# A hybrid decoder trunk: the first layer's splits cut into pieces, and both output projections moved from 256 to 512 columns a matmul

## The chip, the cores and the metric

The kernel runs on one core of a Trainium2 chip. The metric is the device time of one execution in microseconds (us). TensorE (PE in the profile) multiplies; its weight loads (PEld) are rows of their own and overlap the multiplications. VectorE is DVE, ScalarE is ACT, GpSimd is POOL, and SP issues most of the DMA transfers. Each engine works through its own instructions in order and waits on semaphores for the others.

## The reference, cut to what matters

The input is a sequence of 1024 rows of 1024 features in float32. Layer A is a gated DeltaNet, and layer B is a sliding-window attention whose keys and values come from the output of layer A. Both end in an output projection, `x + o @ w_out`, with `o` of 1024 x 2048 and `w_out` of 2048 x 1024. Layer A has 8 heads, and each is a recurrence over chunks of the sequence:

```python
def step(S, inp):
    qk_i, qd_i, kd_i, u_i, w_i, gl_i = inp
    v_new = u_i - jnp.einsum("bhck,bhkv->bhcv", w_i, S)
    o = jnp.einsum("bhck,bhkv->bhcv", qd_i, S) + jnp.einsum("bhcs,bhsv->bhcv", qk_i, v_new)
    S = S * gl_i[..., None, None] + jnp.einsum("bhck,bhcv->bhkv", kd_i, v_new)
    return S, o
```

`kd_i` are the keys times their decay to the chunk's end, and `qk_i` the products of queries and keys times their decay.

## The kernel before

**Split numbers.** A float32 product is made of three matmuls of a faster type (F32R): each operand is split into a rounded part `hi` and the rest `lo`, and hi*hi, hi*lo and lo*hi are added in one PSUM bank. The split of a large tile is one POOL instruction (hi) and one DVE instruction (lo = x - hi), in `split` (L645, L646).

**Layer A, head by head.** `head_delta` (front) writes the recurrence of head h, and the projections of the next head (`head_in`, lines L180, L182 and L184 in `gemm_ct`: 512 columns each) are woven into it as filler. The order of the PE is that of the code. The other engines' instructions are ordered when the program is built, by a scheduler that knows no measured time. A head takes some 104 us. Its parts, in order: the products of queries and keys (L666); an inversion on 64 x 64 blocks (L687, L694); `merge` (L756 to L767); and the scan over 8 chunks n = 0..7.

**The merge and the scan** are where the first half of the change lies. After the merge the decayed keys `kt` (multiplied by `kdec` on POOL in L681) are split into `kth` (tile `w0`) and `ktl` (buffer `lt`), and the products `dm` into `dmh` (tile `w1`) and `dml`. Every chunk then runs a chain over four engines: PE L802 -> ACT L804 (`vh`, buffer `Z`) -> DVE L805 (`vl`, buffer `lh`) -> PE L816 -> DVE L819 or L822 (state `S`) -> PE L793 -> DVE L795 -> PE L802 of the next chunk. L816 of chunk n reads `kth[:, n]`; L652 to L654 read `dmh` and `dml` of the chunk before. The load of the decays of a later head (`dm<-gd`, SP L603) waits for the last reader of the tile; POOL L608 and ACT L612 then work on what it brought.

**The queries** are split into `qh` and `ql` one head ahead, in the same way.

**The output projections** (`out_proj`, called once for each layer) go over 2 halves of the rows and 2 column blocks of 512. Four PSUM tiles, one for each 128 rows, are filled from 8 weight tiles of 512 KB. A weight tile holds 4 row blocks of 128 by 256 columns, and a matmul takes 256 columns:

```python
for kk in range(4):
    nc.tensor.matmul(po, oh[:, kk, ts], hi[:, kk, :], start=(k4 + kk + b == 0), stop=False)
    nc.tensor.matmul(po, oh[:, kk, ts], lo[:, kk, :], start=False, stop=False)
    nc.tensor.matmul(po, ol[:, kk, ts], hi[:, kk, :], start=False, stop=(k4 + kk + b == 7))
```

That is 2 x 2 x 8 x 4 x 4 x 3 = 1536 matmuls for a projection. `weight` loads a tile (SP L125) and splits it on POOL (L150) and DVE (L157), and `weights` names the tiles in order.

Of the kernel before, what the change touches and what calls it, by code (L numbers as in the profile page):

```python
# [7 lines left out]
F32 = mybir.dt.float32  # L8
# [5 lines left out]
ALU = mybir.AluOpType  # L14
# [4 lines left out]
P = 128  # L19
T = 1024  # L20
D = 1024
NB = T // P
# [42 lines left out]
class Kernel:  # L65
# [575 lines left out]
    def split(self, x, ph, hi, pl, lo):  # L641

        nc = self.nc
        hi, lo = (p.tile([P, NB, P], F32R, name=t, bufs=1) for p, t in ((ph, hi), (pl, lo)))
        nc.gpsimd.tensor_scalar(out=hi, in0=x, scalar1=1.0, scalar2=1.0, op0=ALU.mult, op1=ALU.mult)  # L645
        nc.vector.tensor_tensor(out=lo, in0=x, in1=self.f32(hi), op=ALU.subtract)  # L646
        return hi, lo

    def three(self, ps, wh, wl, mh, ml):

# [5 lines left out]
    def head_delta(self, h, H):  # L656
        nc, dl, sm, dps = self.nc, self.dl, self.sm, self.dps
        kq, kt, vt, dm = H.kq, H.kt, H.vt, H.dm
        sh = [P, NB, 64]

        lt = dl.tile([P, NB, P], F32, name="lt", bufs=1)
        for n2 in range(NB // 2):
            ps = dps.tile([P, 2, 2, P], F32, name="kqp")
            for c in range(2):
                n = n2 * 2 + c
                nc.tensor.matmul(ps[:, c, :, :], kq[:, n, 0, :], kq[:, n, :, :], start=True, stop=True)  # L666
            for c in range(2):
                n = n2 * 2 + c
# [7 lines left out]
        for r in (0, 64):  # L676
            nc.scalar.copy(out=lh[r:r + 64, :, :], in_=lt[r:r + 64, :, r:r + 64])
        nc.gpsimd.affine_select(out=lt, in_=lt, pattern=[[0, NB], [1, P]], compare_op=ALU.is_gt, fill=0.0, base=0,
                                channel_multiplier=-1)
        qh, ql = self.split(kq[:, :, 1, :], dl, "qh", dl, "ql")  # L680
        nc.gpsimd.tensor_tensor(out=kt, in0=kt, in1=self.kdec[:, :, h:h + 1].broadcast_to([P, NB, P]), op=ALU.mult)  # L681
        blocks = [(n, r) for n in range(NB) for r in (0, 64)]

        def prod(lhs, rhs):
# [81 lines left out]
            nc.tensor.matmul(ps[0:64, n, :], Zf[64:128, n, :], xt[64:128, n, 64:128], start=True, stop=True)  # L766
        nc.scalar.copy(out=xt[0:64, :, 64:128], in_=ps[0:64, :, :])  # L767
        yield WAIT["merge"]
        kth, ktl = self.split(kt, sm, "w0", dl, "lt")
        dmh, dml = self.split(dm, sm, "w1", dl, "dml")  # L770

        H.o = o = vt
        sso = sm.tile([P, NB], F32, name="sso")
# [15 lines left out]
        for n in range(NB):  # L789
            po[n % 2] = dps.tile([P, 2, 256], F32, name="kqp")  # L790
            if n:
                ps = dps.tile([P, 512], F32, name="sc")[:, 0:256]
                nc.tensor.matmul(ps, kq[:, n, 0, :], S, start=True, stop=True)  # L793
                r = sm.tile(wide, F32, name="r")
                nc.vector.scalar_tensor_tensor(out=r, in0=ps, scalar=self.neG[:, n, h:h + 1], in1=vt[:, n, :],  # L795
                                               op0=ALU.mult, op1=ALU.add)
                inside(n - 1)
                yield WAIT["row"]
            else:
                r = vt[:, n, :]  # L800
            ps = dps.tile([P, 512], F32, name="sc")[:, 0:256]
            nc.tensor.matmul(ps, xt[:, n, :], r, start=True, stop=True)  # L802
            beta = self.beta[:, n, h:h + 1]
            nc.scalar.activation(out=vh, in_=ps, func=AF.Copy, scale=beta)  # L804
            nc.vector.scalar_tensor_tensor(out=vl, in0=ps, scalar=beta, in1=self.f32(vh), op0=ALU.mult,  # L805
                                           op1=ALU.subtract)
            if n:
                self.three(po[n % 2][:, 0, :], qh[:, n, :], ql[:, n, :], Sh, Sl)
                nc.scalar.activation(out=o[:, n, :], in_=po[n % 2][:, 0, :], func=AF.Copy, scale=self.eG[:, n, h:h + 1])
            yield WAIT["new"]  # L810
            if n < NB - 1:
                ps = dps.tile([P, 512], F32, name="sc")[:, 0:256]
                nc.tensor.matmul(ps, kth[:, n, :], vh, start=True, stop=False)
                nc.tensor.matmul(ps, ktl[:, n, :], vh, start=False, stop=False)
                yield WAIT["low"]
                nc.tensor.matmul(ps, kth[:, n, :], vl, start=False, stop=True)  # L816
                S2 = sm.tile(wide, F32, name="S")
                if n:
                    nc.vector.scalar_tensor_tensor(out=S2, in0=S, scalar=self.egl[:, n, h:h + 1], in1=ps,  # L819
                                                   op0=ALU.mult, op1=ALU.add)  # L820
                else:
                    nc.vector.tensor_copy(S2, ps)  # L822
                S = S2
                nc.scalar.copy(out=Sh, in_=S)
                nc.vector.tensor_tensor(out=Sl, in0=S, in1=self.f32(Sh), op=ALU.subtract)
                yield WAIT["state"]
        inside(NB - 1)

# [68 lines left out]
    def out_proj(self, og, resid, cur, tiles, raws, px, acc, dst, finish):  # L897


        nc = self.nc  # L900
        for half in range(2):
            xs, nxt = [], []
            for cp in range(2):
                cs = slice(cp * 512, cp * 512 + 512)
                ps = [acc.tile([P, 2, 256], F32, name="acc") for _ in range(4)]
                for k4 in range(4):
                    oh, ol = cur[k4]
                    for b in range(2):
                        hi, lo = self.take()
                        if cp == 0 and (k4, b) == (2, 0):  # L910
                            self.flush()
                            for c in range(4):
                                xs.append(px.tile([P, D], F32, name="xo", bufs=4))
                                nc.sync.dma_start(xs[c], resid[half * 4 + c])
                        for c in range(4):
                            ts = slice(c * P, c * P + P)
                            po = ps[c][:, b, :]
                            for kk in range(4):
                                nc.tensor.matmul(po, oh[:, kk, ts], hi[:, kk, :], start=(k4 + kk + b == 0), stop=False)  # L919
                                nc.tensor.matmul(po, oh[:, kk, ts], lo[:, kk, :], start=False, stop=False)  # L920
                                nc.tensor.matmul(po, ol[:, kk, ts], hi[:, kk, :], start=False, stop=(k4 + kk + b == 7))  # L921
                                if kk % 2:
                                    self.tick()
                            if (k4, b) == (3, 1):
                                nc.vector.tensor_tensor(out=xs[c][:, cs], in0=ps[c].rearrange("p b c -> p (b c)"),
                                                        in1=xs[c][:, cs], op=ALU.add)
# [413 lines left out]
    def weights(self):  # L1340

        I = self.I
        rows = lambda name: I[name].rearrange("o (k p) c -> p (o k) c", p=P)
        bin_ = rows("b_w_in")
        col = lambda w, b, gain: (w[:, :, b * P:(b + 1) * P], [KT, P], gain)
        four = lambda w, k, c, gain: (w[:, 4 * k:4 * k + 4, c * 256:c * 256 + 256], [4, 256], gain)
        gain = lambda j: self.gcolb[:, 4 * j:4 * j + 4]
        for h in range(AH):
            for b in (8 + h, h, 16 + 2 * h, 17 + 2 * h):
                yield col(self.win, b, None)  # L1350
            if h == 0:
                yield col(self.win, 32, None)
            if h == 1:
                yield col(self.win, 33, None)
            for i in ([h - 1] if h > 1 and h - 1 not in self.late else []) + ([AH - 1, *self.late] if h == AH - 1 else []):
                for b in (32 + 2 * i, 33 + 2 * i):
                    yield col(self.win, b, None)
        for _ in range(2):
            for c in (0, 2):
                for k in range(4):  # L1360
                    for b in range(2):
                        yield four(rows("a_w_out"), k, c + b, None)
        wkv = I["w_kv"].rearrange("(k p) c -> p k c", p=P)
        for c in range(2):
            for k in range(2):
                yield four(wkv, k, c, gain(k))
        for kind, hg, j in self.b_order():
            if kind == "q":
                for k in range(2):
                    yield four(bin_, k, hg, gain(2 + k))  # L1370
            else:
                yield col(bin_, 16 + 2 * hg + j, self.gcolb[:, 8:16])
        for _ in range(2):
            for c in (0, 2):
                for k in range(4):
                    for b in range(2):
                        yield four(rows("b_w_out"), k, c + b, None)

    def dump(self, name, ap):
        self.nc.sync.dma_start(self.dbg[name], ap)  # L1380
# [21 lines left out]
```

## Time and profile before

| | |
|---|---|
| median of 3 runs | 1890.71 us (1887.74 to 1893.08) |
| the profiled execution: its time, its span in the trace | 1894.54 us, 1892.8 us |
| PE busy | 1829.7 us (97%) |
| PEld, DVE, ACT, POOL busy | 1567.2, 1239.6, 838.1, 512.6 us |
| TensorE clock granted, mean | 0.995 |
| projection of layer A | 899.5 to 1089.6 us of the span |
| projection of layer B | 1704.5 to 1888.8 us of the span |

Times inside the trace count from the span's start. A busy PE is not one at its peak: matmuls are pipelined and each shows a duration longer than its distance to the next, so cost is read from the starts of neighbouring rows.

### The profile page before, as it was taken

To read this page: it belongs to the slowest core of one execution; us is meant where nothing else is said; L and a number is where in the kernel's file an instruction comes from. 1 tells how busy PE (TensorE), PEld (TensorE's weight loads), DVE (VectorE), ACT (ScalarE), POOL (GpSimd) and SP (SyncE) were. 2 spreads that over 40 slices of the span, in tenths; PEclk is the share of its full clock that TensorE was granted. 3 is DMA by queue.
4 is the path that set the end of the run, shared out by engine and by line. 5 is a ranking of instruction groups with operands and counts; after the bars stand their busy time and mean duration, and the time that the engine had idled before them with its cause. 6 is when DMAs were issued, how large, how long until landed. Compare 5 with 4: busy or idle time off the path is not lost.

```text
span 1892.8 us, 34012 instructions
## 1 busy us (share of the span) xinstructions
PE 1829.7 (97%) x13186; PEld 1567.2 (83%) x13186; DVE 1239.6 (65%) x3014; ACT 838.1 (44%) x1968; POOL 512.6 (27%) x581
## 2 busy tenths in 40 slices
PE   6999999999999998999999999999999999999999
PEld 5667777787878776778999999888788788879999
DVE  6677776868595878765545366787776776753432
ACT  6446353635445364423011043656756666771100
POOL 0222222322232223221211232333433333321211
PEclk9999999999999999999999999999999999999999
DMA  4611111111111111133654321111211111226542
GB/s 149 143 37 34 56 45 57 34 56 46 34 57 34 46 34 58 33 96 99 229 182 152 112 90 46 42 38 46 67 32 48 56 49 43 73 73 200 188 166 82
DMA packets 151270, 149.74 MB, mean 79 GB/s; under 512 B 7242, under 2 KB 124484, under 8 KB 151108
## 3 DMA queue, kind: packets, MB, share of 16 engines
q1 hardware_dynamic: 140768, 130.40, 22.2%
q10 hardware_dynamic: 10340, 17.16, 2.9%
q8 instruction: 104, 1.70, 0.4%
q14 instruction: 58, 0.48, 0.1%
HBM read 116.05 MB, written 31.49 MB: 78 GB/s over the span
## 4 chain that ended last, share of the span: by engine, by line
PE 68%; DVE 13%; issue 5%; ACT 4%; POOL 3%; DMA 1%; POOLq 0%; ACTq 0%; SPq 0%; DVEq 0%
PE mm L182 8%; PE mm L180 8%; PE mm L184 8%; PE acc L920 6%; PE acc L919 6%; PE acc L921 6%; PE mm L971 4%; PE mm L973 3%; PE mm L972 3%; DVE acc L494 3%; PE pv L1213 2%; DVE wlo L157 2%; PE tp L1192 1%; PE kqp L666 1%; PE lg L1167 1%
## 5 line engine op out<-in xcount | busy, mean ns | idle before, releaser
L180 PE MATMUL mm<-hh,whi 128*128 128x512 f32 (+1 forms) x1040 | 427.2, 411 | 2.6 <-ACT hh L246 2.5
L182 PE MATMUL mm<-hl,whi 128*128 128x512 f32 (+1 forms) x1040 | 417.3, 401 | 1.6 <-DVE hl L247 1.5
L184 PE MATMUL mm<-hh,wlo 128*128 128x512 f32 (+1 forms) x1040 | 415.1, 399 | 0.0
L157 DVE TENSOR_TENSOR wlo<-wraw,whi 128x512 fp32r<-128x512 f32 x292 | 210.8, 749 | 239.4 <-POOL whi L150 214.0
L150 POOL TENSOR_SCALAR whi<-wraw 128x1024 fp32r<-128x1024 f32 x110 | 121.8, 1107 | 493.2 <-PE acc L921 248.3
L180 PEld LDWEIGHTS mm<-hh,whi 128*128 128x128 f32 x1040 | 197.5, 190 | 38.1 <-issue 4.6
L184 PEld LDWEIGHTS mm<-hh,wlo 128*128 128x128 f32 x1040 | 197.1, 190 | 36.0 <-issue 4.2
L182 PEld LDWEIGHTS mm<-hl,whi 128*128 128x128 f32 x1040 | 197.5, 190 | 34.6 <-issue 4.2
L971 PE MATMUL mm<-whi,hh 128*128 128x256 f32 x608 | 179.9, 296 | 0.0
L494 DVE SCALAR_TENSOR_TENSOR acc<-u,cw,acc 128x512 f32<-128x512 f32 x192 | 160.8, 839 | 23.5 <-POOL acc L491 21.0
L973 PE MATMUL mm<-whi,hl 128*128 128x256 f32 x608 | 171.8, 283 | 0.0
L972 PE MATMUL mm<-wlo,hh 128*128 128x256 f32 x608 | 171.7, 282 | 0.0
L919 PE MATMUL acc<-whi,hh 128*128 128x256 f32 x512 | 145.0, 283 | 0.0
L920 PE MATMUL acc<-wlo,hh 128*128 128x256 f32 x512 | 144.9, 283 | 0.0
L921 PE MATMUL acc<-whi,hl 128*128 128x256 f32 x512 | 144.9, 283 | 0.0
L971 PEld LDWEIGHTS mm<-whi,hh 128*128 128x128 f32 x608 | 115.6, 190 | 10.9 <-issue 10.8
L1182 ACT ACTIVATE lsb<-lsb,nm 128x128 f32<-128x128 f32 x256 | 99.8, 392 | 54.6 <-DVE se L1178 44.4
L972 PEld LDWEIGHTS mm<-wlo,hh 128*128 128x128 f32 x608 | 115.8, 190 | 0.2
L973 PEld LDWEIGHTS mm<-whi,hl 128*128 128x128 f32 x608 | 115.5, 190 | 0.0
L920 PE MATMUL acc<-wlo,oh 128*128 128x256 f32 x384 | 108.7, 283 | 1.2 <-DVE wlo L157 1.2
L919 PE MATMUL acc<-whi,oh 128*128 128x256 f32 x384 | 108.6, 283 | 0.0
L921 PE MATMUL acc<-whi,ol 128*128 128x256 f32 x384 | 108.5, 283 | 0.0
(355 smaller groups left out, 4207.0 us busy)
## 6 DMA issues: line engine op xcount, KB each, us to landing
wraw<-in_a_w_in SPq DMA_DIRECT2D x48, 512.0 KB, 4.0
wraw<-in_a_w_out SPq DMA_DIRECT2D x32, 512.0 KB, 4.2
wraw<-in_b_w_in SPq DMA_DIRECT2D x32, 512.0 KB, 4.0
wraw<-in_b_w_out SPq DMA_DIRECT2D x32, 512.0 KB, 3.9
og<-zs SPq DMA_DIRECT2D x32, 256.0 KB, 2.0
ogT<-zs SPq DMA_DIRECT2D x24, 256.0 KB, 2.1
btab<-lt SPq DMA_DIRECT2D x1, 4096.0 KB, 24.2
dm<-gd SPq DMA_DIRECT2D x8, 512.0 KB, 3.7
```

The source lines that it names most:

```text
L150: nc.gpsimd.tensor_scalar(out=hi, in0=raw, scalar1=1.0, scalar2=1.0, op0=ALU.mult, op1=ALU.mult)
L157: nc.vector.tensor_tensor(out=lo[:, ks], in0=raw[:, ks], in1=self.f32(hi[:, ks]), op=ALU.subtract)
L180: nc.tensor.matmul(ps, hi[:, k, :], hh[:, k, :], start=(k == 0), stop=False)
L182: nc.tensor.matmul(ps, hi[:, k, :], hl[:, k, :], start=False, stop=False)
L184: nc.tensor.matmul(ps, lo[:, k, :], hh[:, k, :], start=False, stop=(k == KT - 1))
L494: nc.vector.scalar_tensor_tensor(out=acc, in0=u[:, t:t + 512], scalar=cw[:, t, blk:blk + 1], in1=acc, op0=ALU.mult, op1=ALU.add)
L919: nc.tensor.matmul(po, oh[:, kk, ts], hi[:, kk, :], start=(k4 + kk + b == 0), stop=False)
L920: nc.tensor.matmul(po, oh[:, kk, ts], lo[:, kk, :], start=False, stop=False)
L921: nc.tensor.matmul(po, ol[:, kk, ts], hi[:, kk, :], start=False, stop=(k4 + kk + b == 7))
L971: nc.tensor.matmul(ps, hh[:, k, ts], hi[:, k % 4, :], start=(k == 0), stop=False)
L972: nc.tensor.matmul(ps, hh[:, k, ts], lo[:, k % 4, :], start=False, stop=False)
L973: nc.tensor.matmul(ps, hl[:, k, ts], hi[:, k % 4, :], start=False, stop=(k == KT - 1))
```

## The change

It has two parts. **Splits**: `split` now returns a function `part(hs)` that splits a slice of the 8 chunks. Queries are split and keys decayed in halves. Keys and products are split as chunks 0-1, 2-3 and 4-7; only the first piece of the keys stands in the code ahead of the scan, and the others are called after the state of chunks 0 to 3. **Projections**: a weight tile holds 2 row blocks by 512 columns, and a matmul takes 512.

```diff
+        def part(hs):
+            nc.gpsimd.tensor_scalar(out=hi[:, hs], in0=x[:, hs], scalar1=1.0, scalar2=1.0, op0=ALU.mult, op1=ALU.mult)
+            nc.vector.tensor_tensor(out=lo[:, hs], in0=x[:, hs], in1=self.f32(hi[:, hs]), op=ALU.subtract)
+        return hi, lo, part
...
+        some = (slice(0, 2), slice(2, 4), slice(4, 8))
+        qh, ql, part_q = self.split(kq[:, :, 1, :], dl, "qh", dl, "ql")
+        for hs in (slice(0, 4), slice(4, 8)):
+            part_q(hs)
+            nc.gpsimd.tensor_tensor(out=kt[:, hs], in0=kt[:, hs], in1=self.kdec[:, hs, h:h + 1].broadcast_to([P, 4, P]),
+                                    op=ALU.mult)
...
-        kth, ktl = self.split(kt, sm, "w0", dl, "lt")
-        dmh, dml = self.split(dm, sm, "w1", dl, "dml")
+        kth, ktl, part_k = self.split(kt, sm, "w0", dl, "lt")
+        dmh, dml, part_d = self.split(dm, sm, "w1", dl, "dml")
+        part_k(some[0])
...
+                if n < 4:
+                    (part_d, part_k, part_d, part_d)[n](some[(0, 1, 1, 2)[n]])
+                if n == 2:
+                    part_k(some[2])
...
-                ps = [acc.tile([P, 2, 256], F32, name="acc") for _ in range(4)]
+                ps = [acc.tile([P, 512], F32, name="acc") for _ in range(4)]
...
-                            po = ps[c][:, b, :]
-                            for kk in range(4):
...
+                            for kk in range(2):
+                                k = 2 * b + kk
+                                nc.tensor.matmul(ps[c], oh[:, k, ts], hi[:, kk, :], start=(k4 + k == 0), stop=False)
+                                nc.tensor.matmul(ps[c], oh[:, k, ts], lo[:, kk, :], start=False, stop=False)
+                                nc.tensor.matmul(ps[c], ol[:, k, ts], hi[:, kk, :], start=False, stop=(k4 + k == 6))
+                                self.tick()
...
-            for c in (0, 2):
-                for k in range(4):
-                    for b in range(2):
-                        yield four(rows("a_w_out"), k, c + b, None)
+            for c in (0, 512):
+                for k in range(0, 16, 2):
+                    yield rows("a_w_out")[:, k:k + 2, c:c + 512], [2, 512], None
```

The built programs show where the pieces land. **DVE, end of the merge of head 1, before:** `acc` is a convolution of the next head, `lt<-kt` and `dml<-dm` are the splits, and `lh<-sc` is L805 of chunk 0.

```order
L494 SCALAR_TENSOR_TENSOR acc<-u,cw,acc 128x512 x2
L646 TENSOR_TENSOR lt<-kt,w_2667 128x1024
L646 TENSOR_TENSOR dml<-dm,w_2671 128x1024
L805 SCALAR_TENSOR_TENSOR lh<-sc,beta,Z 128x256
L553 TENSOR_TENSOR part<-tr,cst 128x16
```

The same place in the changed program (L648 is the split there, and L812 is L805):

```order
L494 SCALAR_TENSOR_TENSOR acc<-u,cw,acc 128x512
L648 TENSOR_TENSOR lt<-kt,w_2681 128x256 x2
L494 SCALAR_TENSOR_TENSOR acc<-u,cw,acc 128x512
L648 TENSOR_TENSOR lt<-kt,w_2681 128x512
L648 TENSOR_TENSOR dml<-dm,w_2683 128x256 x2
L648 TENSOR_TENSOR dml<-dm,w_2683 128x512
L812 SCALAR_TENSOR_TENSOR lh<-sc,beta,Z 128x256
L553 TENSOR_TENSOR part<-tr,cst 128x16
```

All six pieces stand ahead of the chunk's own instruction, as the two whole splits did; heads 2, 3 and 4 read the same. **DVE, the same place in head 5, before:** `kt<-kt,rky` belongs to the next head.

```order
L591 TENSOR_TENSOR kt<-kt,rky 128x1024
L646 TENSOR_TENSOR lt<-kt,w_7030 128x1024
L494 SCALAR_TENSOR_TENSOR acc<-u,cw,acc 128x512
L646 TENSOR_TENSOR dml<-dm,w_7034 128x1024
L805 SCALAR_TENSOR_TENSOR lh<-sc,beta,Z 128x256
```

And in the changed program:

```order
L591 TENSOR_TENSOR kt<-kt,rky 128x1024
L648 TENSOR_TENSOR lt<-kt,w_7088 128x256 x2
L648 TENSOR_TENSOR lt<-kt,w_7088 128x512
L648 TENSOR_TENSOR dml<-dm,w_7090 128x256 x2
L494 SCALAR_TENSOR_TENSOR acc<-u,cw,acc 128x512
L648 TENSOR_TENSOR dml<-dm,w_7090 128x512
L812 SCALAR_TENSOR_TENSOR lh<-sc,beta,Z 128x256
```

Here too nothing moved behind the chunk's instruction. Head 7 reads alike, but one weight split (`wlo`) that stood ahead of it now stands behind it; in head 0 the last piece of `dml` stands behind it. **POOL, the end of the merge of head 1, in the changed program** (the pieces of the keys are on L647, the decay on L686):

```order
L686 TENSOR_TENSOR kt<-kt,kdec 128x512 x2
L647 TENSOR_SCALAR w_2681<-kt 128x256 x2
L647 TENSOR_SCALAR w_2681<-kt 128x512
L647 TENSOR_SCALAR w_2683<-dm 128x256 x2
L647 TENSOR_SCALAR w_2683<-dm 128x512
L150 TENSOR_SCALAR whi<-wraw 128x1024
```

Before, the same places held one instruction each of 128x1024 for `kt`, `w<-kt` and `w<-dm`. On the PE nothing changed its place; each projection has half the matmuls, of 128x512.

## Rows read from the trace of the kernel before

**Rows 1.** Page, part 1: busy us, share of the span, instructions.
```profile
PE 1829.7 (97%) x13186; PEld 1567.2 (83%) x13186; DVE 1239.6 (65%) x3014; ACT 838.1 (44%) x1968; POOL 512.6 (27%) x581
```
**Rows 2.** Busy time by stretch: the projection of layer B.
```profile
core 0: us, PE busy (x) PEld busy (x) DVE busy (x) ACT busy (x) POOL busy (x), PEclk, DMA share, GB/s
1704.50:1888.80 184.30, 184.30 (x1538) 184.30 (x1536) 67.61 (x90) 14.02 (x15) 32.59 (x30) 1.00 0.49 160
```
**Rows 3.** Timeline of PE, projection of layer B: start, duration, engine, line.
```profile
1800.07 0.28 PE L920 MATMUL acc<-wlo,hh 128*128 128x256 f32 x1
...
1802.47 0.28 PE L919 MATMUL acc<-whi,hh 128*128 128x256 f32 x1
```
**Rows 4.** Timeline of PE, end of head 1: unbroken run of 512 columns.
```profile
294.04 0.39 PE L180 MATMUL mm<-hh,whi 128*128 128x512 f32 x1
...
302.20 0.39 PE L180 MATMUL mm<-hh,whi 128*128 128x512 f32 x1
```
**Rows 5.** Timeline of PE, end of layer B's attention: a shorter run.
```profile
1690.72 0.39 PE L180 MATMUL mm<-hh,whi 128*128 128x512 f32 x1
...
1694.21 0.40 PE L180 MATMUL mm<-hh,whi 128*128 128x512 f32 x1
```
**Rows 6.** Who waited for whom on PE, the longest: us, times, longest.
```profile
PE sc L816 <- DVE lh L805: 12.7, 15, 1.9
```
**Rows 7.** Timeline of POOL, merge of head 1.
```profile
244.75 1.91 POOL L681 TENSOR_TENSOR kt<-kt,kdec 128x1024 f32<-128x1024 f32 x1 [1.21 <-PE tr L596]
246.63 1.48 POOL L645 TENSOR_SCALAR w<-kt 128x1024 fp32r<-128x1024 f32 x1
248.78 1.90 POOL L645 TENSOR_SCALAR w<-dm 128x1024 fp32r<-128x1024 f32 x1 [0.67 <-PE kqp L766]
```
**Rows 8.** Timeline of DVE, merge of head 1.
```profile
244.99 3.66 DVE L494 SCALAR_TENSOR_TENSOR acc<-u,cw,acc 128x512 f32<-128x512 f32 x2
248.57 1.21 DVE L646 TENSOR_TENSOR lt<-kt,w 128x1024 fp32r<-128x1024 f32 x1
250.72 1.23 DVE L646 TENSOR_TENSOR dml<-dm,w 128x1024 fp32r<-128x1024 f32 x1 [0.94 <-POOL w L645]
251.86 0.47 DVE L805 SCALAR_TENSOR_TENSOR lh<-sc,beta,Z 128x256 fp32r<-128x256 f32 x1
```
**Rows 9.** Timeline of DVE, shortly after: neighbours without POOL beside them.
```profile
254.33 0.41 DVE L825 TENSOR_TENSOR XT<-S,X 128x256 fp32r<-128x256 f32 x1
254.67 0.47 DVE L795 SCALAR_TENSOR_TENSOR r<-sc,neG,vt 128x256 f32<-128x256 f32 x1
255.06 0.73 DVE L494 SCALAR_TENSOR_TENSOR acc<-u,cw,acc 128x512 f32<-128x512 f32 x1
255.72 0.68 DVE L157 TENSOR_TENSOR wlo<-wraw,whi 128x512 fp32r<-128x512 f32 x1
256.32 1.57 DVE L494 SCALAR_TENSOR_TENSOR acc<-u,cw,acc 128x512 f32<-128x512 f32 x1
```
**Rows 10.** POOL by line: duration in ns, least, median and most.
```profile
L1137 POOL TENSOR_SCALAR qh<-qr x64: 398/407/851, 1160.5 to 1660.4; 128x256 fp32r<-128x256 f32 x64
L491 POOL TENSOR_SCALAR acc<-u,cw x64: 687/697/1640, 34.0 to 797.3; 128x512 f32<-128x512 f32 x64
L645 POOL TENSOR_SCALAR qh<-kq x8: 1046/1046/1057, 58.1 to 793.8; 128x1024 fp32r<-128x1024 f32 x8
L1186 POOL TENSOR_TENSOR lsb<-lsb,den x64: 1035/1042/2105, 1178.9 to 1695.0; 128x512 f32<-128x512 f32 x64
```
**Rows 11.** Timeline of PE, head 1: chunk 0 and chunk 1.
```profile
252.67 0.36 PE L816 MATMUL sc<-lh,w 128*128 128x256 f32 x1
...
258.20 0.39 PE L813 MATMUL sc<-Z,w 128*128 128x256 f32 x1 [0.45 <-ACT Z L804]
```
**Rows 12.** Timelines of SP and ACT, head 1: the decays of a later head.
```profile
251.97 0.34 SPq L603 DMA_DIRECT2D dm<-gd  x1
...
257.39 0.40 ACT L612 ACTIVATE dm<-dm,mG 128x128 f32<-128x128 f32 x1 [0.49 <-POOL dm L608]
```

More of the change, by code (lines that the diff above doesn't have):

```diff
@@ L644, in split @@
         hi, lo = (p.tile([P, NB, P], F32R, name=t, bufs=1) for p, t in ((ph, hi), (pl, lo)))
-        nc.gpsimd.tensor_scalar(out=hi, in0=x, scalar1=1.0, scalar2=1.0, op0=ALU.mult, op1=ALU.mult)
-        nc.vector.tensor_tensor(out=lo, in0=x, in1=self.f32(hi), op=ALU.subtract)
-        return hi, lo
+        def part(hs):
+            nc.gpsimd.tensor_scalar(out=hi[:, hs], in0=x[:, hs], scalar1=1.0, scalar2=1.0, op0=ALU.mult, op1=ALU.mult)
+            nc.vector.tensor_tensor(out=lo[:, hs], in0=x[:, hs], in1=self.f32(hi[:, hs]), op=ALU.subtract)
+        return hi, lo, part
     def three(self, ps, wh, wl, mh, ml):
@@ L679, in head_delta @@
                                 channel_multiplier=-1)
-        qh, ql = self.split(kq[:, :, 1, :], dl, "qh", dl, "ql")
-        nc.gpsimd.tensor_tensor(out=kt, in0=kt, in1=self.kdec[:, :, h:h + 1].broadcast_to([P, NB, P]), op=ALU.mult)
+        some = (slice(0, 2), slice(2, 4), slice(4, 8))
[4 more added lines that the diff above has]
+                                    op=ALU.mult)
         blocks = [(n, r) for n in range(NB) for r in (0, 64)]
@@ L916, in out_proj @@
                             ts = slice(c * P, c * P + P)
-                            po = ps[c][:, b, :]
-                            for kk in range(4):
[L919 to L923, printed above, removed]
+                            for kk in range(2):
[4 more added lines that the diff above has]
+                                self.tick()
                             if (k4, b) == (3, 1):
-                                nc.vector.tensor_tensor(out=xs[c][:, cs], in0=ps[c].rearrange("p b c -> p (b c)"),
-                                                        in1=xs[c][:, cs], op=ALU.add)
+                                nc.vector.tensor_tensor(out=xs[c][:, cs], in0=ps[c], in1=xs[c][:, cs], op=ALU.add)
                                 nc.sync.dma_start(dst[half * 4 + c][:, cs], xs[c][:, cs])
@@ L1373, in weights @@
         for _ in range(2):
[L1374 to L1377, printed above, removed]
+            for c in (0, 512):
+                for k in range(0, 16, 2):
+                    yield rows("b_w_out")[:, k:k + 2, c:c + 512], [2, 512], None
     def dump(self, name, ap):
```

## The prediction

> **What bounds the kernel now.** The page comes first: PE is busy for 97% of the span [rows 1], so time is won where the PE's matmuls get cheaper, or where it waits for others. Which of the two holds is read stage by stage, and the change touches two stages with different answers.
>
> In the projection of layer B, PE and PEld are both busy for all of the 184.3 us [rows 2]; nothing else ends last there, and POOL and DVE, who split the weights, have time to spare (32.6 and 67.6 us). The pace is 20 matmuls of 256 columns in 2.40 us, 0.120 us each, read from start to start [rows 3]; 1536 of them make 184.3 us, the whole stretch. The projection of layer A, 190.1 us by the table, is the same 184.3 us with transposes of the next norm and short waits in between.
>
> In the scan of layer A the list of waits is the view to read. Its longest entry on the PE is L816 waiting for DVE's L805: 12.7 us in 15 waits, the longest 1.9 us [rows 6]. L816 needs `vl`, and DVE makes it only after what stands ahead in its queue: the splits, in chunk 0. So the scan pays for DVE's order, and the split's length matters where L805 is late.
>
> **The projections.** The change takes out 1536 pairs (768 in each projection) of 256-column matmuls, with their weight loads, and puts one of 512 columns for each. The trace has 512 columns in `gemm_ct`. In the longest unbroken run, 36 of them take 8.16 us, 0.2267 each [rows 4]; in a shorter run in layer B, 15 take 3.49 us, 0.2327 each [rows 5]. A pair takes 0.240, so the gain is 13.3 ns or 7.3 ns for a pair, 20.5 us or 11.2 us for 1536. I take the first, because a projection is a run without breaks, as in rows 4, and round it to 19 us, because the one in layer A is interrupted. The work around it stays hidden: a weight tile is still 512 KB and 1024 elements a partition for POOL and DVE, now needed every 24 x 0.2267 = 5.44 us in place of 48 x 0.120 = 5.76. By the stretch's totals DVE has 67.6 us of work in 184.3 and POOL 32.6; 20 us less leaves both far from full. If that cover were gone, the PE would wait for `wlo`.
>
> The Trainium skill (TensorE: Matmul & The Clock Gate, Back-to-back issue gap) gives a distance of columns / 2.4 plus 2.5 ns at the full clock, 109 ns and 216 ns here; by it a pair would gain 2.5 ns and the two projections 3.8 us. The rows show 120 and 227, some 13 ns above columns / 2.4 in both, and I go by the rows; what follows if the page were right is the second rival.
>
> **The scan.** What the code says and what the built program does differ here. The later pieces are written behind the first chunks, but DVE's order puts all of them ahead of L805 (L812 in the new lines) in heads 1 to 6, with the same neighbours; in head 7 one weight split moves behind it, in head 0 the last piece of `dml`. So nothing is taken out of L805's way in most heads, and the pieces cost more than the whole.
>
> How much more: DVE's next instruction starts 0.34 us after one of 256 columns and 0.60 after one of 512 [rows 9], and 1.14 after one of 1024 [rows 8]. Three pieces take 0.34 + 0.34 + 0.60 = 1.28, 0.14 more. On POOL, 256, 512 and 1024 columns last 0.41, 0.70 and 1.05 [rows 10], and a next one starts 0.03 before the end (1.91 long, 1.88 to the next [rows 7]): 0.38 + 0.38 + 0.67 - 1.02 = 0.41 more for a split, and for the decay in halves (1.04 each [rows 10]) 2 x 1.01 - 1.88 = 0.14 more.
>
> Does POOL's part add to DVE's? In head 1 two convolution steps that take 0.66 each from start to start [rows 9] last 3.66 us together [rows 8], just while POOL works on `kt` and `w` [rows 7], and POOL's `w<-dm`, 1.05 long alone, lasts 1.90 beside DVE's `lt`. The two engines take turns. From 244.75 the sum of both is 1.88 + 1.02 + 1.02 on POOL and 2 x 0.66 + 2 x 1.14 on DVE, 7.5 us, or 252.3; L805 starts at 251.86, 0.4 us earlier. So I add them: 0.14 (decay) + 0.41 + 0.14 (keys) + 0.41 + 0.14 (products) = 1.24 us later in heads 1 to 4.
>
> There L805 ends at 252.33 and L816 starts at 252.67 [rows 8, 11]: the first 0.34 us are free, and 0.9 reach the PE in chunk 0. The rest comes back in chunk 1: the load of decays that waits for `dml` is issued at 251.97, 0.02 us after `dml` ends, ACT's L612 waits for its result until 257.39 [rows 12], and behind L612 stands the L804 for which the PE waits 0.45 us at 258.20 [rows 11]. I take 1.1 us for each of four heads, 4.4 us. In heads 5 and 6 the decay is not in this chain and L816 waits already, so all of 1.10 counts: 2.2 us. Head 7 gains 0.60 from the weight split and head 0 as much from the piece: 0.5 us each. Sum: 7.6 us; I take 7.5. The halves of the queries add 0.3 us at the end of the scan, where DVE and POOL wait for the PE and hide it.
>
> Bounds: if pieces could overlap between the engines after all, DVE would have 0.60 in place of 1.14 left after POOL's last piece, 0.54 us earlier in all heads, -4 us. Upwards, 1.5 us in each of 8 heads (1.24, with some for more turns) is +12.
>
> **The sum.** -19 + 7.5 = -11.5 us. The profiled execution took 1894.5 us for a span of 1892.8, and would take 1883.0; the median of the runs is 3.8 us below it, so the median goes from 1890.7 to **1879.2 us**.
>
> **Rivals.** (1) *The pieces overlap.* DVE begins with the first piece while POOL rounds the next, and `dml` is done earlier: -19 - 4, 1867.7 us. For it: DVE's first piece needs POOL's first alone. Against it: the turns in rows 7 and 8. Chance 0.12.
>
> (2) *A matmul costs by its columns alone.* Then 512 columns take 2 x 0.120, the projections gain nothing and the scan still loses: 1890.7 + 7.5 = 1898.2 us, slower. It decides when the distance of two starts is 0.235 or more (a gain of under 7.7 us). For it: nothing but single distances of 0.23 to 0.24 in rows 5. Against it: rows 4. With the gain by the Trainium skill's rule above the time would be 1894.4. Chance 0.05.
>
> (3) *The scan loses more than the projections give.* One place, the chain POOL, DVE, L816 in the merge: from 2.4 us a head it eats the 19 us, and from 3.1 us a head the kernel is measurably slower, e.g. 1897 us at 3.2. Against it: twice the summed cost of the pieces. Chance 0.06.
>
> (4) *512 columns at the pace of rows 5.* -11.2 + 7.5: 1887.0 us. Chance 0.12.
>
> **The numbers.** My forecast has 0.65, with a range of its own of 1873 to 1885 us (17 to 20.5 gained, 3 to 11 lost). A difference of 0.3%, 5.7 us, is about what runs of this kernel can tell from none: faster is below 1885.0, slower above 1896.4. Faster: 0.62 of the forecast, 0.12 of (1) and 0.02 of (4), 0.76. Slower: 0.04 of (2), 0.05 of (3), 0.09. Same: the rest, 0.15. The range that leaves out no more than 2 in 10 goes from 1869, near (1), to 1889, past (4).
>
> **What would show it.** Projections: matmul starts 0.227 us apart, layer B's stretch of 184.3 us down to some 174, no new entry for `wlo` in PE's waits. Scan: the entry L816 <- L805 (with the new lines) grows from 12.7 us to between 16 and 20, and in head 1 L805 of chunk 0 starts 1.0 to 1.3 us later against the PE's last L766. I am wrong in the projections if the starts are 0.232 or more apart, and in the scan if that entry shrinks: then the pieces do overlap, or the turns between POOL and DVE cost less than their sum.

## The result, and the profile after

The changed kernel takes 1875.0 us (median of 4 runs, 1873.5 to 1875.3); the kernel before, on the same chip, 1891.9. The ratio is 0.9913, with a 95% interval of 0.9895 to 0.9930: 13 to 20 us faster. The forecast was 1879.2.

The profiled execution of the changed kernel took 1873.5 us for a span of 1871.8, 21.0 less than before; the one of before lay 2.6 us above its median. Page, part 1, of the changed kernel, beside [rows 1]:

```profile
PE 1810.5 (97%) x11650; PEld 1485.2 (79%) x11650; DVE 1239.5 (66%) x3054; ACT 838.5 (45%) x1968; POOL 529.0 (28%) x629
```

PE has the 1536 matmuls less; POOL 48 instructions and 16 us more. Since PE's order is the same up to the first projection, its starts can be laid side by side, and they split the 21.0 us: layer A up to its projection 3.6, that projection with the keys' projection behind it 6.0, the attention 1.3, the projection of layer B 10.3 (0.1 is lost behind it). The last, busy time by stretch, beside [rows 2], and two PE rows 12 matmuls apart, beside [rows 3]:

```profile
1693.58:1867.82 174.24, 174.24 (x770) 144.07 (x768) 66.07 (x90) 14.41 (x15) 32.24 (x30) 1.00 0.51 168
```
```profile
1788.94 0.39 PE L931 MATMUL acc<-whi,hh 128*128 128x512 f32 x1
...
1791.66 0.39 PE L931 MATMUL acc<-whi,hh 128*128 128x512 f32 x1
```

2.72 us for 12 is 0.2267 each, 174 us for the stretch: both as predicted. Layer A's projection is another picture. Its timeline on PE, every third matmul, first inside one weight tile and then inside the next:

```profile
913.79 0.39 PE L931 MATMUL acc<-whi,oh 128*128 128x512 f32 x1
...
918.69 0.39 PE L931 MATMUL acc<-whi,oh 128*128 128x512 f32 x1
...
922.14 0.39 PE L931 MATMUL acc<-whi,oh 128*128 128x512 f32 x1
...
924.18 0.39 PE L931 MATMUL acc<-whi,oh 128*128 128x512 f32 x1
```

21 matmuls in 4.90 us are 0.2333 each, 9 in 2.04 are 0.2267. Two of every three weight tiles run at the first pace, one at the second, all the way.

In the scan, PE's longest waits, beside [rows 6]: the entry shrank, where the prediction had it grow to 16 to 20 us.

```profile
PE sc L823 <- DVE lh L812: 10.8, 14, 2.2
...
PE sc L820 <- ACT Z L811: 2.5, 4, 1.1
...
PE sc L800 <- DVE S L826: 1.6, 3, 1.2
```

The merge of head 1 on POOL and DVE, beside [rows 7, 8]:

```profile
244.62 2.52 POOL L686 TENSOR_TENSOR kt<-kt,kdec 128x512 f32<-128x512 f32 x2 [0.78 <-PE tr L596]
247.12 1.52 POOL L647 TENSOR_SCALAR w<-kt 128x256 fp32r<-128x256 f32 x3
249.10 2.30 POOL L647 TENSOR_SCALAR w<-dm 128x256 fp32r<-128x256 f32 x3 [0.45 <-PE kqp L772]
```
```profile
247.56 1.36 DVE L648 TENSOR_TENSOR lt<-kt,w 128x256 fp32r<-128x256 f32 x2 [1.32 <-POOL w L647]
248.84 0.74 DVE L494 SCALAR_TENSOR_TENSOR acc<-u,cw,acc 128x512 f32<-128x512 f32 x1
249.50 0.88 DVE L648 TENSOR_TENSOR lt<-kt,w 128x512 fp32r<-128x512 f32 x1
250.31 1.97 DVE L648 TENSOR_TENSOR dml<-dm,w 128x256 fp32r<-128x256 f32 x3
252.19 0.47 DVE L812 SCALAR_TENSOR_TENSOR lh<-sc,beta,Z 128x256 fp32r<-128x256 f32 x1
```

The reader is to see four things. POOL still waits for L772 (L766 before) ahead of `w<-dm`, 0.45 us in place of 0.67, so what decay and keys cost more is over by then; `w<-dm` starts 0.38 us after the start of the last L772 in both kernels. DVE begins `lt` at 247.56, 0.44 after POOL's first piece, where it began at 248.57. And from the start of POOL's `w<-dm` to L812 it is 3.09 us, before 251.86 - 248.78 = 3.08. The fourth stands on ACT, in the same head, before and after:

```profile
248.68 0.63 ACT L575 ACTIVATE acc<-acc 128x512 f32<-128x512 f32 x1 [1.86 <-DVE acc L494]
249.34 0.58 ACT L767 COPY xt<-kqp 64x512 f32<-64x512 f32 x1
```
```profile
248.98 0.58 ACT L773 COPY xt<-kqp 64x512 f32<-64x512 f32 x1 [1.84 <-PE kqp L772]
249.61 0.63 ACT L575 ACTIVATE acc<-acc 128x512 f32<-128x512 f32 x1
```

The copy of `xt` (L767, now L773), which the first matmul of the scan reads, stood behind a step of the convolution (L575) and stands ahead of it now, so it starts 0.26 us after the start of the last L772 in place of 0.94.

### The profile page after: what moved, and what is told of

Read it like the earlier page. It is cut to its first block, busy times and chain, and to the rows that moved or that the text cites. A ratio compares the mean times of both kernels' runs of the same rounds, so it can differ in the third digit from the quotient of the medians.

```text
span 1871.8 us, 31061 instructions
## 1 busy us (share of the span) xinstructions
PE 1810.5 (97%) x11650; PEld 1485.2 (79%) x11650; DVE 1239.5 (66%) x3054; ACT 838.5 (45%) x1968; POOL 529.0 (28%) x629
## 4 chain that ended last, share of the span: by engine, by line
PE 68%; DVE 13%; issue 4%; POOL 4%; ACT 3%; DMA 1%; POOLq 0%; ACTq 0%; SPq 0%; DVEq 0%
PE mm L180 8%; PE mm L182 8%; PE mm L184 8%; PE acc L933 6%; PE acc L932 6%; PE acc L931 6%; PE mm L981 3%; PE mm L983 3%; PE mm L982 3%; DVE acc L494 2%; PE pv L1223 2%; DVE wlo L157 2%; PE kqp L693 1%; PE sc L800 1%; PE kqp L668 1%
## 5 line engine op out<-in xcount | busy, mean ns | idle before, releaser
L157 DVE TENSOR_TENSOR wlo<-wraw,whi 128x512 fp32r<-128x512 f32 x292 | 206.0, 732 | 217.3 <-POOL whi L150 191.9
L494 DVE SCALAR_TENSOR_TENSOR acc<-u,cw,acc 128x512 f32<-128x512 f32 x192 | 152.7, 797 | 22.0 <-POOL acc L491 19.7
L491 POOL TENSOR_SCALAR acc<-u,cw 128x512 f32<-128x512 f32 x64 | 56.9, 890 | 183.7 <-ACT u L487 162.0
L1196 POOL TENSOR_TENSOR lsb<-lsb,den 128x512 f32<-128x512 f32 x64 | 67.9, 1061 | 136.1 <-ACT pT L1206 50.8
L153 POOL TENSOR_TENSOR wraw<-wraw,gcolb 128x512 f32<-128x512 f32 x72 | 80.8, 1143 | 88.5 <-DMA wraw<-in_b_w_in 52.5
L931 PE MATMUL acc<-whi,hh 128*128 128x512 f32 x256 | 99.7, 390 | 0.0
L933 PE MATMUL acc<-whi,hl 128*128 128x512 f32 x256 | 99.6, 389 | 0.0
L932 PE MATMUL acc<-wlo,hh 128*128 128x512 f32 x256 | 99.6, 389 | 0.0
```

The source lines that it names most:

```text
L157: nc.vector.tensor_tensor(out=lo[:, ks], in0=raw[:, ks], in1=self.f32(hi[:, ks]), op=ALU.subtract)
L494: nc.vector.scalar_tensor_tensor(out=acc, in0=u[:, t:t + 512], scalar=cw[:, t, blk:blk + 1], in1=acc, op0=ALU.mult, op1=ALU.add)
L931: nc.tensor.matmul(ps[c], oh[:, k, ts], hi[:, kk, :], start=(k4 + k == 0), stop=False)
L932: nc.tensor.matmul(ps[c], oh[:, k, ts], lo[:, kk, :], start=False, stop=False)
L933: nc.tensor.matmul(ps[c], ol[:, k, ts], hi[:, kk, :], start=False, stop=(k4 + k == 6))
```

## The experiments

Two tables help with several of them. The first gives, worked out from the timelines, the start of chunk 0's L812 after the start of the last L772 (L805 and L766 in the lines of before), in us:

```
                         head 0   1     2     3     4     5     6     7
before                   4.11   3.46  3.46  3.47  3.65  4.33  4.99  4.47
changed kernel           3.79   3.47  3.48  3.48  3.46  4.53  5.18  3.90
e3 pieces in place       3.73   3.41  3.41  3.41  3.82  4.52  5.12  3.89
e4 pieces behind         2.32   3.04  3.01  3.02  3.01  4.06  4.05  2.56
e8 whole                 4.12   3.21  3.22  3.18  3.62  4.33  4.99  4.47
e9 eight pieces          3.84   5.02  5.00  5.02  5.44  4.40  5.06  4.62
e10 hi whole             4.46   3.50  3.50  3.50  3.96  4.61  5.27  4.57
```

The second gives the same for L823 (L816 before), the PE's first matmul that reads what L812 makes:

```
                         head 0   1     2     3     4     5     6     7     sum
before                   4.65   4.27  4.27  4.26  4.45  4.87  5.53  5.01  37.3
changed kernel           4.33   4.01  4.00  4.03  4.01  5.07  5.72  4.43  35.6
e3 pieces in place       4.26   4.07  4.08  4.08  4.69  5.06  5.66  4.43  36.3
e4 pieces behind         2.98   4.49  4.47  4.46  4.46  4.60  4.59  3.48  33.5
e8 whole                 4.66   4.63  4.64  4.60  5.03  4.87  5.53  5.01  39.0
e9 eight pieces          4.38   6.22  6.21  6.44  6.65  4.93  5.60  5.16  45.6
e10 hi whole             5.00   4.79  4.77  4.79  5.25  5.14  5.81  5.11  40.7
```

In heads 0, 5, 6 and 7 the PE stands idle until L812 has run (in e4 in heads 5 and 6 only). In heads 1 to 4 it has no idle time right before L823 in any of these kernels: there L812 is done before the PE comes to L823.

All ratios below are to the kernel before, measured beside the experiment (medians 1891.4 for e1 to e4, 1891.7 for e5 to e8, 1890.3 for e9 and e10).

### e1: the projections alone

The kernel before with the new `out_proj` and `weights`, and the old `split`.

> The kernel before with the second half of the change alone: weight tiles of 2 row blocks by 512 columns and matmuls of 512 columns in both output projections; the splits stay whole. The prediction's term: 19 us faster than before, some 1872 us. What the two traces showed since: layer B's projection gave 10.3 us as predicted, layer A's 6 to 7.5 of its 9.5, so 16 to 18 us, some 1874 us. Rival (a matmul costs by its columns alone): no gain. If the rest of layer A is where the result came from, this kernel stays under 14 us.

1877.6 us, ratio 0.9923 (0.9909 to 0.9936): 12 to 17 us. In its trace layer B's projection is 10.3 us shorter and layer A's stretch 6.0, to the tenth as in the changed kernel. The projections carry the result, with less than the 19 us of the prediction.

### e2: the pieces alone

The changed `split` and `head_delta`, with the projections of before.

> The kernel before with the first half of the change alone: splits and decays in pieces; the projections keep their 256 columns. The prediction's term: 7.5 us slower, some 1898 us, with the PE's wait L816 <- L805 (new lines L823 <- L812) grown from 12.7 us to 16 to 20. The theory after the traces (a piece on DVE starts after one piece on POOL, so the pieces run beside each other and the handover costs less than it gains): 2 to 4 us faster, some 1888 us, and that entry at 10 to 12 us. Rival (layer A's 3.6 us came from the clock and from chance): within 1.5 us of before with the entry unchanged.

1890.3 us, ratio 0.9991 (0.9982 to 1.0001): between 3.4 us faster and 0.2 slower. The wait list of PE has

```profile
PE sc L823 <- DVE lh L812: 11.0, 15, 2.2
```

Plus 7.5 us is excluded, minus 4 too. By the second table L823 comes 1.7 us earlier in the changed kernel, over eight heads (e2 has the same starts within 0.02 us); that fits both this interval and the rest of the result. 0.9 us of it are heads 0 and 7, where L812 is earlier; heads 5 and 6 lose 0.4; the other 1.2 are heads 1 to 4, where L812 is not earlier and not waited for, and come from the order on ACT shown above.

### e3: the pieces, none behind a chunk

```diff
-        part_k(some[0])
+        [p(hs) for p in (part_k, part_d) for hs in some]
...
-                if n < 4:
-                    (part_d, part_k, part_d, part_d)[n](some[(0, 1, 1, 2)[n]])
-                if n == 2:
-                    part_k(some[2])
```

> The changed kernel with all six pieces of keys and products written ahead of the scan, none behind the first chunks; in the built order of DVE only one convolution step per head changes its place among the pieces, and in head 0 the last piece of the products comes ahead of the first chunk. Theory (the pieces help by overlapping, not by standing behind the chunks): the same time as the changed kernel within 1.5 us, some 1875 us. Rival (the code's order is what helps): 2 to 4 us slower than the changed kernel, 1877 to 1879 us, with the wait of the PE for DVE's L812 back at 12 us or more.

1875.4 us, ratio 0.9907 (0.9892 to 0.9922), the wait for L812 11.2 us. As the built order of DVE said, the place of the calls in the code does nothing here that this run can tell.

### e4: the pieces really behind the chunks

DVE's later pieces and L812 of chunks 0 to 3 (L813 in this kernel) are held in the order of the code:

```diff
-            nc.vector.scalar_tensor_tensor(out=vl, in0=ps, scalar=beta, in1=self.f32(vh), op0=ALU.mult,
-                                           op1=ALU.subtract)
+            keep = self.tc.keep_in_program_order if n < 4 else lambda i: i
+            keep(nc.vector.scalar_tensor_tensor(out=vl, in0=ps, scalar=beta, in1=self.f32(vh), op0=ALU.mult, op1=ALU.subtract))
...
-                    (part_d, part_k, part_d, part_d)[n](some[(0, 1, 1, 2)[n]])
+                    keep((part_d, part_k, part_d, part_d)[n](some[(0, 1, 1, 2)[n]]))
...
-                    part_k(some[2])
+                    keep(part_k(some[2]))
```

> The changed kernel with DVE's order fixed: the later five pieces really stand behind L812 of chunks 0 to 3, as the code was written. If the pieces ahead of L812 are what the PE still waits for in chunk 0 (heads 0, 5, 6 and 7: 6 of the 10.8 us of that wait), 3 to 6 us faster than the changed kernel, 1869 to 1872 us, and the wait for L812 at 5 to 8 us. Rival (the wait only moves: DVE then works on the pieces inside the scan, where r, S and L812 of the next chunks stand behind them, and the decays of the next head are loaded later): the same or slower, 1875 to 1880 us, with new waits for r, S or dml of several us.

1887.3 us, ratio 0.9983 (0.9972 to 0.9994): 12 us slower than the changed kernel. The wait did move. PE's list:

```profile
PE kqp L655 <- DVE dml L648: 10.4, 15, 1.1
PE sc L823 <- DVE lh L813: 8.5, 10, 1.7
```

L812 is earlier in every head (the table), by 0.4 us in heads 1 to 4, and the wait for it shrank by 2.3 us. In its place stands 10.4 us of L655, which reads `dml` one chunk later and finds it unfinished, two times in most heads. In heads 1 to 4 L823 comes 0.4 to 0.5 us later than in the changed kernel although L812 is earlier: in this build ACT's L575 stands ahead of the copy of `xt` again. What the code intended loses.

### e5: the same weight tiles, 256 columns a matmul

```diff
+                                for j, cc in enumerate((slice(0, 256), slice(256, 512))):
+                                    po = ps[c][:, cc]
+                                    nc.tensor.matmul(po, oh[:, k, ts], hi[:, kk, cc], start=(k4 + k + j == 0), stop=False)
...
```

> The changed kernel with its weight tiles of 2 row blocks by 512 columns, but each matmul of the projections again cut in two of 256 columns: the order of transfers, splits and blocks is that of the change, the count of matmuls that of before. Theory (the projections gain a fixed 13 ns for each matmul taken out): all of it comes back, layer B's projection at 184.3 us, both together 16 us slower than the changed kernel, some 1891 us. Rival (the shape of the weight tiles and the order of the blocks give the gain): layer B's projection stays at 174 us and the time at 1875 us.

1888.7 us, ratio 0.9988 (0.9977 to 0.9999). Layer B's projection:

```profile
1702.30:1886.71 184.41, 184.41 (x1538) 184.36 (x1536) 65.12 (x90) 14.37 (x15) 31.30 (x30) 1.00 0.46 159
```

All 10 us are back. In layer B the gain belongs to the count of matmuls (each with its weight load; no run separates the two), not to the tiles' shape or order. Layer A's projection takes 188.8 us from its first matmul to the first of the keys' weights, 1.4 less than before and 6.1 more than in the changed kernel: of its gain 6.1 go with the count, and 1.4 with the tiles, as a wait for `wlo` shrinks.

### e6: layer B's weights high in SBUF

The addresses of the built program suggest what the two paces of layer A's projection are. Its activations lie at 155 to 221 KB of a partition of SBUF, the memory that the PE reads its operands from (1 KB is 1000 bytes here). Its weight tiles rotate over three places: two at 28 to 45 KB and one at 131 to 139 KB. The tiles at 131 KB are those at 0.2267. In layer B weights (28 to 45 KB) and activations (45 to 110 KB) are both low. This run takes the weights alone up:

```diff
                     px = pool(c2, "px2", 2)
+                    wr = pool(c2, "wr", 2, side="right")
+                    self.wpools = [wr]
```

> The changed kernel with the weight tiles of layer B's projection in two buffers at the high end of SBUF, the activations where they were (44 to 110 KB). Theory (512 columns run at 226.7 ns where both operands lie low or both high, and at 233.3 where one lies low and the other high): all of layer B's projection goes to 700 ns for three matmuls, its stretch from 174.0 to 179.1 us, and the kernel is 5 us slower than the changed one, some 1880 us. Rival (layer A's projection is slower for the work beside it, transfers and splits, and not for the place of its operands): 680 ns for three matmuls and 174.0 us as before.

1885.2 us, ratio 0.9967 (0.9954 to 0.9980). PE's timeline inside the projection, 12 matmuls apart:

```profile
1714.70 0.40 PE L931 MATMUL acc<-whi,hh 128*128 128x512 f32 x1
...
1717.51 0.40 PE L931 MATMUL acc<-whi,hh 128*128 128x512 f32 x1
```

2.81 us, 0.234 each, and so it stays to the end. The first two weight tiles still lie low, and run at 0.2267. The stretch grew by 8.9 us: 5.5 are this pace, and 3.4 are one wait at its start, where DVE's split of the first high tile (L157) starts only at 1708.48 us, behind splits of activations (L907) that wait for their data. The place theory holds; the time of the whole kernel, 10 us above the changed one's where 5 were expected, was missed for the most part by that wait.

### e7: layer A's weights high in SBUF

The residual rows (`xo`, 16 KB) borrow the place of `kn` and `vv`, which are written later, and the weights get three `whi` and two `wlo` buffers beside the activations; every third `wlo` stays low.

```diff
-                    self.wpools, self.wcount, self.depth = [self.wsp, wx, self.wsp], 1, 2
+                    self.wpools, self.wcount, self.depth = [High()] * 31 + [wsp] * 9, 0, 2
...
+                            if name == "wlo" and turn.count(name) % 3 == 0:
+                                return wsp.tile(shape, dt, name=name)
+                            return wx.tile(shape, dt, name=name, bufs=3 if name == "whi" else 2)
```

> The changed kernel with the weight tiles of layer A's projection high in SBUF, beside its activations (155 to 221 KB), from the second tile on (one wlo of three stays low); the residual rows lie in the place of the keys and values of layer B in the meantime. Theory (place of the operands): the 20 of 32 weight tiles that took 5.60 us take 5.44 or, with a low wlo, 5.50; layer A's projection is 2.5 to 3.3 us shorter than in the changed kernel (182.7 us from its first matmul to the first of the keys' weights), and the kernel as much faster, 1872 to 1873 us. Rival (work beside it sets the pace): no change. Rival (the borrowed place of the residual rows makes the keys' projection wait): that gain is lost in new waits behind 1075 us.

1869.0 us, ratio 0.9880 (0.9867 to 0.9892): faster than both kernels. The first L931 of four weight tiles in a row, from PE's timeline:

```profile
955.39 0.39 PE L931 MATMUL acc<-whi,oh 128*128 128x512 f32 x1
...
960.83 0.39 PE L931 MATMUL acc<-whi,oh 128*128 128x512 f32 x1
...
966.38 0.40 PE L931 MATMUL acc<-whi,oh 128*128 128x512 f32 x1
...
971.86 0.39 PE L931 MATMUL acc<-whi,oh 128*128 128x512 f32 x1
```

5.44, then 5.55 with the low `wlo`, then 5.48 for the tile behind it: all three are faster than the 5.60 to 5.62 of the low tiles in the changed kernel. From its first matmul to the first of the keys' weights the projection takes 180.3 us, 2.4 less than in the changed kernel, a little under what was expected. The medians differ by more, some 6 us, and so do the traces: 1.8 us ahead of the projection, which the edit does not touch, and 2.7 behind it. In both places the changed kernel's granted clock has a stretch at one half (0.50 from 105.6 to 109.0 us, 0.51 from 1088.6 to 1092.1), and this one's has none; the first makes 1.4 of the 1.8 us. The first is no effect of the buffers: e6, which leaves this part alone too, was granted 1.00 there as well. Whether the second is, no run separates.

### e8: keys and products whole

```diff
-        part_k(some[0])
+        [p(slice(0, 8)) for p in (part_k, part_d)]
```

with the calls behind the chunks taken out, as in e3.

> The changed kernel with the splits of keys and products whole again, ahead of the scan; queries and decay stay in halves. The prediction's working (pieces cost 0.55 us for each split on POOL and DVE together, and both engines' parts add up): 1.1 us in each of 8 heads come back, up to 7 us faster than the changed kernel, 1868 to 1871 us. The theory after the traces (DVE's last piece is short, and that pays for POOL's longer work): the same to 2 us slower, 1875 to 1877 us.

1875.8 us, ratio 0.9920 (0.9907 to 0.9933). The 7 us that the prediction's working had for these pieces are not there, and 2 us are below what this run can tell. The tables show more: with whole splits L812 comes 0.3 us earlier than in the changed kernel in heads 1 to 3, and L823 0.6 later, because the PE waits for `Z` there (3.3 us in its list, 2.5 in the changed kernel's), which has nothing to do with L812; e10 shows the way.

### e9: eight pieces

```diff
-        part_k(some[0])
+        [p(slice(n, n + 1)) for p in (part_k, part_d) for n in range(NB)]
```

> The changed kernel with keys and products split in eight pieces of one chunk each (128 columns), all ahead of the scan; it is compared with the three pieces in place (1875.4 us). Carrying on the steps of 256 and 512 columns (DVE 0.34 and 0.60, POOL 0.38 and 0.67), 128 would take 0.21 and 0.235, so eight take 0.40 more on DVE and 0.45 more on POOL than three. The prediction's working (both engines' parts add up): 1.7 us later in each of 8 heads, some 12 us slower, 1887 us. The theory of the overlap (POOL's longer work counts, DVE's only by its last piece, which is 0.39 shorter): 0.5 us later in each head, most of it inside the free third of a microsecond in heads 1 to 4, 1875 to 1878 us.

1885.6 us, ratio 0.9975 (0.9965 to 0.9984): 10 us slower than e3 by the medians and 13 by the ratios, as the prediction's working would have it, but not by its mechanism. DVE in head 1, where the last L772 starts at 247.22:

```profile
248.48 2.35 DVE L648 TENSOR_TENSOR dml<-dm,w 128x128 fp32r<-128x128 f32 x8
250.75 1.57 DVE L494 SCALAR_TENSOR_TENSOR acc<-u,cw,acc 128x512 f32<-128x512 f32 x1
252.24 0.47 DVE L812 SCALAR_TENSOR_TENSOR lh<-sc,beta,Z 128x256 fp32r<-128x256 f32 x1
```

`dml` ends 3.60 us after that L772, against 3.49 in e3, though POOL ends 0.65 later: the pieces overlap, and 16 of them cost a tenth. But in this build a convolution step stands between `dml` and L812 and takes 1.57 us, so L812 comes 1.6 later in heads 1 to 4 (the table), and PE's longest entry is now L525 waiting for ACT's L575, 10.4 us in place of 1.8; L575 waits for that convolution step. Behind these waits the clock fell to a half in each of heads 1 to 3, where it did not in e3. My own expectation missed that: I had counted pieces and not looked at what stands behind them.

### e10: hi whole, lo in pieces

```diff
-        part_k(some[0])
+        for x, hi, lo in ((kt, kth, ktl), (dm, dmh, dml)): [nc.gpsimd.tensor_scalar(out=hi, in0=x, scalar1=1.0, scalar2=1.0, op0=ALU.mult, op1=ALU.mult)] + [nc.vector.tensor_tensor(out=lo[:, hs], in0=x[:, hs], in1=self.f32(hi[:, hs]), op=ALU.subtract) for hs in some]
```

> The changed kernel with the rounded parts of keys and products made by one POOL instruction each, and only DVE's rests in three pieces, ahead of the scan: the pieces cost DVE 0.14 us a split, and none can start before POOL has done the whole. Theory of the overlap (what pays is that DVE begins after POOL's first piece): in head 1 L812 of chunk 0 starts 0.2 to 0.4 us later against the PE than in the kernel before the change, with DVE's tail behind POOL's last instruction at 1.2 us in place of 0.8; by the clock of the whole kernel no difference that can be told from the three pieces in place, 1874 to 1878 us. Rival (POOL's three pieces are what cost, and their overlap gives nothing): L812 earlier than with the pieces in place by 0.4 us in each head, 1872 us.

1880.7 us, ratio 0.9942 (0.9924 to 0.9960): 5 us slower than e3 by the medians and 7 by the ratios, more than expected, and the rival's gain is absent. From the last instruction of POOL to L812 it is 1.73 us in head 1 (0.80 in e3), but POOL ends earlier by as much, and L812 itself is later by only 0.1 us there (the table). PE's wait list has 13.2 us for L812 and 4.1 for `Z`, 4.0 us more together than the changed kernel's. The second table says where: L823 comes 4.3 us later than in e3 over eight heads. 1.4 of them are heads 0 and 7, where L812 is later and the PE waits for it; 2.7 are heads 1 to 4, where the PE waits for `Z` (L811). ACT in head 1:

```profile
253.44 0.63 ACT L575 ACTIVATE acc<-acc 128x512 f32<-128x512 f32 x1 [1.50 <-DVE acc L494]
253.98 0.46 ACT L811 ACTIVATE Z<-sc,beta 128x256 fp32r<-128x256 f32 x1
```

L811 stands behind the convolution's L575, and that waits for DVE's L494, which runs late behind the pieces of `lt`. The whole of layer A up to its projection is 7.5 us longer than in e3's trace; the other 3 us go with the clock, granted at a half in four stretches there, in e3 in two.

## Why the prediction was right, and where it was not

**The bound and the projections: right, one half mis-sized.** Layer B's projection gave 10.3 us, the 10.25 that 768 pairs at 13.3 ns make, and e5 shows that the count is what paid. The rule of the Trainium skill (TensorE: Matmul & The Clock Gate, Back-to-back issue gap), which the prediction set beside it and which that section gives for a matmul by itself, makes an estimate of 768 x 2.5 ns = 1.9 us there; the trace does not agree with it. The term that was off is the other half: "-19", rounded down from 20.5 for interruptions. Layer A's projection, 190.2 us from its first matmul to the first of the keys' weights, took 182.7, a gain of 7.5. The reason is not an interruption: 504 of its 768 matmuls (21 of 32 weight tiles) ran at 0.2333, which costs 504 x 6.67 ns = 3.4 us, the 11 other tiles begin at that pace and lose 0.04 us each, 0.4 together, and a wait for `wlo` of 1.2 us that stood in the kernel before is gone (10.25 - 3.4 - 0.4 + 1.2 = 7.6). The pace of [rows 5], which I had kept for a rival and taken for a matter of a run's length, applied to two thirds of this stage, by the place of its operands (e6, e7).

**The scan: wrong.** +7.5 us were predicted; e2 gives -1.1 (-3.4 to +0.2), no loss, and by the traces a gain of 1.7. The step that failed is "So I add them: ... = 1.24 us later in heads 1 to 4". L812 came 0.01 us later in head 1, not 1.0 to 1.3. Two things are wrong in the sum, and one was not looked at:

- 0.69 of the 1.24 us (decay and keys) stood before a wait. [Rows 7] showed it: POOL waits 0.67 us for L766 before `w<-dm`. What POOL does more ahead of that only shortens the wait, and the chain to L805 begins anew at L766.
- Behind it the products' pieces do cost POOL the 0.41 that I had: its last one ends 2.67 us after L772 starts, before 2.28. But DVE then has only its last piece to do: from there to L812 it is 0.80 us in place of 1.18. That is the mechanism of rival (1), and against the kernel before it pays for POOL exactly. I had named it, and set "the turns" against it; e9 shows that even 16 pieces move the end of `dml` by only 0.11 us. A gain by itself it is not: against the whole splits of e8 the pieces make L812 0.3 us later in heads 1 to 3 and 0.2 in heads 5 and 6, and 0.3 and 0.6 earlier in heads 0 and 7; over all eight heads they are 0.15 us later.
- In heads 1 to 4 the PE does not wait for L805 in chunk 0 at all: L816 has no idle time before it [rows 11], and L823 has none. It comes 0.23 to 0.44 us earlier because ACT's copy of `xt` now stands ahead of L575. The working follows POOL, DVE and the PE, and takes ACT in only for chunk 1.

In heads 5 and 6, where "all of 1.10 counts", it was 0.20 and 0.19. In heads 7 and 0, taken as +0.5 each, L812 came 0.57 and 0.32 earlier. What was right there is the reading of DVE's built order: e3 shows that the calls behind the chunks do nothing, and e4 that doing as they say costs 12 us.

**The sum.** -17.8 (10.3 + 7.5) for the projections and -1.7 for the scan make -19.5 by the traces, against the -11.5 predicted, and -16.5 (13 to 20) by the medians. Some of the profiled executions' 21.0 is the clock: the kernel before was granted 0.51 from 675.4 to 678.9 and 0.50 from 1576.6 to 1580.0 us, the changed one 1.00 at the first place, and 0.51 in a new one, from 1088.6 to 1092.1. Along the PE's starts each such stretch costs 1.4 to 1.6 us. The new one stands at the same place of the work in the traces of seven of the ten experiments, e1's among them; with it the projections give 16.3 us, which e1's interval of 12 to 17 holds, where 17.8 lies outside. So the time came out in the range in part by luck: 9 us too pessimistic in the scan, and 1 us too optimistic in the projections.

**The rivals.** (1) was right in that the pieces overlap, not in its size: it would have given 4 us beside 19. (2) and (3) fall with e5 and e2. (4) came true for two thirds of one projection.

## What to carry to other kernels

A cost in a producer counts only from the last wait for something outside the chain; add up a chain from that point, and ask of a split what the consumer still has to do behind the producer's last piece. Read the built order before believing where code puts work, and what stands between the work and the instruction that is waited for: one convolution step there cost more than ten extra pieces. Before pricing a wait, see that the engine stands idle right before the instruction in question: in four of eight heads here it did not, and what moved the PE there was the order on an engine whose instructions the change does not touch. When the trace shows two paces for one kind of instruction, find out which operands belong to which before choosing one for the sum.

## What the runs showed of the hardware that was not expected

- Matmuls of 512 columns start 0.2267 us apart where weight and activation tiles both lie below 111 KB of a partition, or both from 131 KB up, and 0.2333 to 0.2342 where one lies low and the other high (layer A's projection, e6). The places are read from the built programs. With only `wlo` apart the tile takes 5.55 us in place of 5.44 (e7). 256 columns show 0.120 either way (before and e5, in both projections). Where between 111 and 131 KB a limit lies, or whether it is one address at all, was not tried; nor is reading the weights there told apart from writing them there.
- Behind a tile at the slow pace the next one's first nine matmuls take 0.231 us each, and 0.2267 from then on (5.48 in place of 5.44 us for the tile, in the changed kernel and in e7), so the first matmuls of a run do not tell its pace.
- The granted clock fell to a half (1.2 in place of 2.4 GHz) behind some of the PE's waits and not behind others of like length: in the kernel before it fell at 675.46 us, where a wait of 1.94 us for L805 ended; in the changed kernel a wait of 2.14 us for L812 ended at 662.21, and the clock stayed at 1.00. From one kernel's trace to the next it can differ in a part that is the same in both: at 105.6 us it was a half in the changed kernel and 1.00 in e3, e6 and e7.
